# Weight products walked from the last column to the first

## The chip, the cores and the metric

The kernel runs on one core of one Trainium2 chip. The metric is the device time of one execution in microseconds. The kernel before took 2161.43 us as the median of three executions (2161.38 to 2162.55 us).

## The reference

A two-layer decoder trunk on 256 tokens of width 2048, all in float32. With `rms` for the scaled root-mean-square norm, it computes:

```
x = x + NSA(rms(x))                       # 16 heads: compressed, selected and window branch, gated
x = x + square(relu(rms(x) @ up0)) @ down0    # up: 2048 x 8192, down: 8192 x 2048
k, v = rms(x) @ kv_w_shared               # once
x = x + DiffAttn(rms(x) @ w_q, k, v) @ w_out  # softmax minus lambda times softmax
x = x + square(relu(rms(x) @ up1)) @ down1
out = rms(x)
```

Nearly all of its arithmetic is in the products of 256 tokens with weight matrices: 64 MB for each of the four MLP matrices, and 5168, 2048, 1024, 2048 and 2048 columns of 2048 rows for the projections.

## The kernel before, in words

**Split operands.** A float32 operand is held as two float32r tiles, a high part and a low part (`split`, L149: ScalarE copies the high part, VectorE subtracts it from the source). A product is three TensorE products: high by high, high by low, low by high (`mm3`, L144).

**Weights.** `plan` lists the weight matrices in units of 512 rows by 512 columns. A unit is read by two DMAs of 512 KB on SyncE's queue into `raw` tiles (L266) and split into two pairs `wh`, `wl` of 128 partitions x 2 x 512 (L151 and L152). Up to four units are asked for ahead, and two split ahead (`advance`, L283). `raw`, `wh` and `wl` have four buffers each.

**Two product loops use a unit.** `unit_mm` (L296) serves the projections, the two output products and the down products: for each of four row blocks and both token blocks it holds 128 x 128 of the activations stationary and streams 512 weight columns through `mm3`, 24 products of 512 columns in all. They add up in two PSUM tiles of 512 columns, one for each token block. `up_unit` (L709) serves the up products: it holds 128 x 128 of the weights stationary and streams the activations of one row block. Those lie as 256 high and 256 low columns side by side, so the product with `wh` streams 512 columns and that with `wl` the first 256, into the same PSUM tile; a unit has 16 such pairs, over four PSUM tiles.

**What else uses TensorE.** The products of the compression (`cmp_units`, L511), of the gates (L483) and of attention (`nsa_head`, `diff_head`) call `mm` and `mm3` directly. `transpose` (L140) turns tiles against an identity.

**Order.** TensorE's and SyncE's instructions stand in the order in which the program issues them. Attention's steps are put between the weight products by a planner: each `mm` adds `max(o.shape[-1], 256) / 2400.0` us to a model clock (L138), and `tick` starts the next waiting step when its due time has come. PSUM has eight tiles of 512 columns, four named `acc` and four named `tp`.

Of the kernel before, what the change touches and what calls it, by code (L numbers as in the profile page):

```python
# [16 lines left out]
S = 256  # L17
# [14 lines left out]
def kernel(  # L32
# [79 lines left out]
    def tick():  # L112
        if tasks and tasks[0][0] <= clock[0]:
            step()
# [21 lines left out]
    def mm(o, l, r, start, stop, shared=False):  # L136
        nc.tensor.matmul(o, lhsT=l, rhs=r, start=start, stop=stop, skip_group_check=shared)  # L137
        clock[0] += max(o.shape[-1], 256) / 2400.0  # L138

    def transpose(o, i, idn):  # L140
        nc.tensor.transpose(o, i, idn)  # L141
        clock[0] += 0.11

    def mm3(o, lh, ll, rh, rl, start, stop):  # L144
        mm(o, lh, rh, start, False)
        mm(o, lh, rl, False, False)
        mm(o, ll, rh, False, stop)
# [148 lines left out]
    def unit_mm(us, ps, lhs, start, stop, ts_=(0, 1)):  # L296
        for kk in range(4):
            wh, wl = us[kk // 2]
            h, l = lhs(kk)
            for t in ts_:  # L300
                ts = slice(t * P, (t + 1) * P)
                mm3(ps[t], h[:, ts], l[:, ts], wh[:, kk % 2, :], wl[:, kk % 2, :],
                    start and kk == 0, stop and kk == 3)
                tick()

# [18 lines left out]
    def xt_chunk(c, sets):  # L324
        for pr in range(2):
            if pr:
                yield 0.8
            tp = PT("tp")
            for kk in range(2):
                k = pr * 2 + kk  # L330
                for t in range(2):
                    transpose(tp[:, kk * 256 + t * P:kk * 256 + (t + 1) * P],
                                        x[c][:, t, k * P:(k + 1) * P], ident)
            for gf, xt in sets:
                for kk in range(2):
                    k = c * 4 + pr * 2 + kk
                    split(xt[k // 8][:, k % 8, 0, :], xt[k // 8][:, k % 8, 1, :],
                          tp[:, kk * 256:(kk + 1) * 256], gf(k))
# [25 lines left out]
    def transpose_k(src, th, tl):  # L364

        for pr in range(2):
            if pr:
                yield 0.8
            tp = PT("tp")
            for hh in range(2):  # L370
                for t in range(2):
                    h = pr * 2 + hh
                    transpose(tp[:, hh * 256 + t * P:hh * 256 + (t + 1) * P],
                              src[:, t, h * P:(h + 1) * P], ident)
            hs = slice(2 * pr, 2 * pr + 2)
            split(th[:, hs], tl[:, hs], tp.rearrange("p (h t q) -> p h t q", h=2, t=2))
# [19 lines left out]

    tp = PT("tp")
    transpose(tp[:, 0:32], grow_a, ident[0:32, 0:32])
    nc.vector.tensor_copy(gcol, tp[:, 0:32])
    gsub = cp.tile([P, 1], F32, name="gsub")  # L400
# [23 lines left out]
    def proj(xt, between=None, before=None):  # L424
        ps = [PT("acc"), PT("acc")]
        for u in range(4):
            if before is not None:
                drain(before[u])
                tick()
            unit_mm(next_unit(), ps, xtlhs(xt, 4 * u), u == 0, u == 3)  # L430
            if between is not None:
                between(u)
        return ps
# [29 lines left out]
    for j in range(2):  # L463
        ps = proj(xt, before=None if j else xts)
# [46 lines left out]
    def cmp_units(j, cps, first):  # L511
        def f(u):
            drain(tX[j])
            us = next_unit()
            for kk in range(4):
                l = first * 4 + u * 4 + kk
                wh, wl = us[kk // 2]
                mm(cps[0:120, :], X[j][:, l, :], wh[:, kk % 2, :], l == 0, False)
                mm(cps[0:120, :], X[j][:, l, :], wl[:, kk % 2, :], False, l == 31)
                tick()  # L520
        return f
# [57 lines left out]
    for j in range(2):  # L579
        cps = PT("acc")  # L580
        ps = proj(xt, cmp_units(j, cps, 0))
        ready.append(spawn(project_k(ps, kkh[:, :, j::2, :], kkl[:, :, j::2, :])))
        tick()
        ps = proj(xt, cmp_units(j, cps, 4))
# [90 lines left out]
    for g in range(4):  # L675
        ps = proj(xt)
# [11 lines left out]
    def out_proj(oth, otl, sets, ss):  # L688
        done = []
        pss = {}  # L690
        for c, g in out_order():
            while len(line) < 4 * g + 4:
                clock[0] = max(clock[0], tasks[0][0])
                step()
            drain(*line[4 * g:4 * g + 4])
            if (c, g) in OUT_FIRST:
                pss[c] = [PT("acc"), PT("acc")]
            ps = pss[c]
            unit_mm(next_unit(), ps, xlhs(oth, otl, 4 * g), (c, g) in OUT_FIRST, (c, g) in OUT_LAST)
            if (c, g) in OUT_LAST:  # L700
                for t in range(2):
                    nc.vector.tensor_tensor(x[c][:, t, :], x[c][:, t, :], ps[t], ALU.add)
            if g == 3:
                done.append(spawn(xt_chunk(c, sets()), 3.5))
                stat_chunk(ss, c)
        line.clear()
        return done

    def up_unit(us, ps, xt, k0):  # L709


        for pair in range(2):
            for kk in range(4):
                wh, wl = us[kk // 2]
                k = k0 + kk
                both = xt[k // 8][:, k % 8].rearrange("p s q -> p (s q)")
                for b in (2 * pair, 2 * pair + 1):
                    bs = slice(b * P, (b + 1) * P)
                    mm(ps[b], wh[:, kk % 2, bs], both, k == 0, False)
                    mm(ps[b][:, 0:S], wl[:, kk % 2, bs], both[:, 0:S], False, k == 15)  # L720
                tick()

    def mlp(layer, xt, rs, last_hook, before):
        r2 = T([P, 2], "nrs")
        nc.vector.tensor_tensor(r2, rs, rs, ALU.mult)
        for G in range(4):
            hid = []
            for c in range(4):
                ps = [PT("acc" if c % 2 == 0 else "tp") for _ in range(4)]
                for u in range(4):  # L730
                    if G == 0 and c == 0:
                        drain(before[u])
                        tick()
                    up_unit(next_unit(), ps, xt, 4 * u)
                r = T([P, 4, S], "q")
                h = new_kv(2, 4, S)
                for b in range(4):
                    nc.scalar.activation(r[:, b, :], ps[b][:, S:2 * S], AF.Copy)
                    nc.vector.tensor_tensor(r[:, b, :], r[:, b, :], ps[b][:, 0:S], ALU.add)
                    nc.vector.scalar_tensor_tensor(r[:, b, :], r[:, b, :], 0.0, r[:, b, :], ALU.max, ALU.mult)  # L740
                    split(h[:, 0, b, :], h[:, 1, b, :], r[:, b, :])
                hid.append(h)
# [8 lines left out]
            for c, u in down_order(final):  # L751
                if u == 0:
                    tag = "tp" if c >= 2 and G < 3 else "acc"
                    pss[c] = [PT(tag), PT(tag)]
                lhs = xlhs(hid[u][:, 0], hid[u][:, 1], 0)
                if final and c >= 2 and u == 3:
                    kept[c] = (next_unit(), lhs)
                    continue
                unit_mm(next_unit(), pss[c], lhs, u == 0, u == 3)
                if u == 3:  # L760
                    for t in range(2):
                        residual(c, t)
                    if G == 3:
                        last_hook(c)
# [49 lines left out]
    ps = proj(kxt, before=xts)  # L814
# [5 lines left out]
    for d in (dkh, dkl):  # L820
        for cc in range(2):
            r = slice(64 - cc * 64, 128 - cc * 64)
# [19 lines left out]
    ps = proj(kxt)  # L842
# [83 lines left out]
    for g in range(4):  # L926
        ps = proj(dxt)
# [100 lines left out]
```

## Time and profile before

| | |
|---|---|
| median of three executions | 2161.43 us |
| the profiled execution | 2163.18 us |
| span, first to last instruction, of that execution | 2161.4 us |
| TensorE products | 10780 instructions, busy 2133.4 us |
| VectorE, ScalarE, GpSimd busy | 1334.9, 1083.1, 82.4 us |
| read from HBM | 390.47 MB, 182 GB/s over the span |

The span lies inside the execution's own time, which is 1.8 us longer. Busy time of TensorE counts a product from its start to its modelled end, so that products in a row overlap; how fast they follow each other is read from a stretch's length over the count of products in it. The granted clock stands as a share of full speed.

### The profile page before, as it was taken

Reading aid. Unit: us, or ns where it says so; the run is one execution under the profiler, and the core shown is the slowest. Engines: PE = TensorE matmul, PEld = TensorE weight load, DVE = VectorE, ACT = ScalarE, POOL = GpSimd, SP = SyncE. Lnnn points to the kernel's source line nnn. Section 1 sums busy time; section 2 is a strip of 40 time slices with the busy share of each in tenths; the row PEclk is TensorE's granted clock in tenths of the full one; section 3 lists DMA queues with packets and bytes.
Section 4 is the critical chain, followed back from the end, with each engine's and each line's share of the span. In section 5 each row is a group of like instructions: output and inputs, shape, how many; then the busy total and the mean of one; then the engine's idle time right before and its main releaser. Section 6 shows DMA issues by size and latency. Waiting matters only on the chain.

```text
span 2161.4 us, 28803 instructions
## 1 busy us (share of the span) xinstructions
PE 2133.4 (99%) x10780; PEld 1797.2 (83%) x10780; DVE 1334.9 (62%) x2156; ACT 1083.1 (50%) x1737; POOL 82.4 (4%) x121
## 2 busy tenths in 40 slices
PE   8999999999999999999999999999999999999998
PEld 6778888888888888888888877888888888888886
DVE  5666777675546555555666578866555655655654
ACT  6565666464435434434455466655434434534443
POOL 0101100000000000000000111000000000000000
PEclk9999999999999999999999999999999999999999
DMA  7788432456666566566565644466666666666654
GB/s 238 236 264 249 124 102 89 149 175 195 194 188 184 195 194 183 192 193 189 181 194 185 189 142 127 132 192 187 198 192 185 191 194 186 185 195 186 192 190 143
DMA packets 204828, 394.45 MB, mean 183 GB/s; under 512 B 14176, under 2 KB 14368, under 8 KB 204560
## 3 DMA queue, kind: packets, MB, share of 16 engines
q1 hardware_dynamic: 203936, 390.51, 58.2%
q0 software_dynamic: 560, 2.02, 0.3%
q8 instruction: 84, 1.38, 0.3%
q14 instruction: 56, 0.46, 0.1%
q10 hardware_dynamic: 192, 0.08, 0.0%
HBM read 390.47 MB, written 2.10 MB: 182 GB/s over the span
## 4 chain that ended last, share of the span: by engine, by line
PE 92%; DVE 3%; DMA 2%; ACT 1%; issue 1%; POOL 0%; DVEq 0%; SPq 0%; POOLq 0%; ACTq 0%
PE acc L137 57%; PE tp L137 33%; PE tp L141 2%; DVE wl L152 1%; DMA raw<-in_nsa_w_in_dram 1%; DMA raw<-in_nsa_cmp_w_dram 1%; ACT wh L151 1%; ACT sbt L879 0%; ACT sa L879 0%; POOL sq L915 0%; DVE sbt L886 0%; DVE big L155 0%; DVE psl L152 0%; DVE sa L886 0%; DVE pwl L911 0%
## 5 line engine op out<-in xcount | busy, mean ns | idle before, releaser
L152 DVE TENSOR_TENSOR wl<-raw,wh 128x1024 fp32r<-128x1024 f32 x736 | 903.7, 1229 | 712.0 <-ACT wh L151 706.8
L151 ACT ACTIVATE wh<-raw 128x1024 fp32r<-128x1024 f32 x736 | 778.2, 1059 | 827.1 <-PE acc L137 488.0
L137 PE MATMUL acc<-wh,big 128*128 128x512 f32 (+1 forms) x1600 | 542.7, 400 | 1.9 <-ACT wh L151 1.9
L137 PE MATMUL acc<-wh,kv 128*128 128x512 f32 x1280 | 397.0, 390 | 0.0
L137 PE MATMUL tp<-big,wh 128*128 128x512 f32 (+1 forms) x1040 | 362.8, 395 | 0.0
L137 PE MATMUL acc<-big,wh 128*128 128x512 f32 x1024 | 361.7, 397 | 0.0
L137 PEld LDWEIGHTS acc<-wh,big 128*128 128x128 f32 (+1 forms) x1600 | 301.6, 189 | 61.3 <-ACT wh L151 2.3
L137 PE MATMUL acc<-wl,big 128*128 128x512 f32 (+1 forms) x832 | 326.3, 392 | 0.5 <-DVE wl L152 0.5
L137 PE MATMUL tp<-big,wl 128*128 128x256 f32 (+1 forms) x1040 | 289.4, 281 | 0.0
L137 PE MATMUL acc<-big,wl 128*128 128x256 f32 x1024 | 287.4, 281 | 0.0
L137 PEld LDWEIGHTS acc<-wh,kv 128*128 128x128 f32 x1280 | 240.3, 188 | 50.0
L137 PE MATMUL acc<-wl,kv 128*128 128x512 f32 x640 | 249.1, 389 | 0.0
L137 PE MATMUL tp<-wh,kv 128*128 128x512 f32 x768 | 237.4, 389 | 0.0
L137 PEld LDWEIGHTS tp<-big,wh 128*128 128x128 f32 (+1 forms) x1040 | 194.2, 187 | 46.7
L137 PEld LDWEIGHTS acc<-big,wh 128*128 128x128 f32 x1024 | 192.2, 188 | 46.3
L137 PEld LDWEIGHTS tp<-big,wl 128*128 128x128 f32 (+1 forms) x1040 | 195.4, 189 | 0.0
L137 PEld LDWEIGHTS acc<-big,wl 128*128 128x128 f32 x1024 | 193.5, 189 | 0.2
L137 PEld LDWEIGHTS acc<-wl,big 128*128 128x128 f32 (+1 forms) x832 | 157.0, 189 | 28.7 <-DVE wl L152 1.0
L137 PEld LDWEIGHTS tp<-wh,kv 128*128 128x128 f32 x768 | 144.1, 188 | 30.0
L137 PE MATMUL tp<-wl,kv 128*128 128x512 f32 x384 | 149.4, 389 | 0.0
L137 PEld LDWEIGHTS acc<-wl,kv 128*128 128x128 f32 x640 | 120.2, 188 | 24.5
L151 ACT ACTIVATE kv<-q 128x256 fp32r<-128x256 f32 x128 | 50.0, 412 | 73.4 <-DVE q L740 73.4
(183 smaller groups left out, 1418.1 us busy)
## 6 DMA issues: line engine op xcount, KB each, us to landing
raw<-in_mlp_w_up_dram SPq DMA_DIRECT2D x256, 512.0 KB, 3.9
raw<-in_mlp_w_down_dram SPq DMA_DIRECT2D x256, 512.0 KB, 4.3
raw<-in_nsa_w_in_dram SPq DMA_DIRECT2D x80, 512.0 KB, 4.5
raw<-in_nsa_cmp_w_dram SPq DMA_DIRECT2D x32, 512.0 KB, 4.9
raw<-in_nsa_w_out_dram SPq DMA_DIRECT2D x32, 512.0 KB, 3.7
raw<-in_diff_w_q_dram SPq DMA_DIRECT2D x32, 512.0 KB, 3.7
raw<-in_diff_w_out_dram SPq DMA_DIRECT2D x32, 512.0 KB, 3.7
raw<-in_kv_w_shared_dram SPq DMA_DIRECT2D x16, 512.0 KB, 3.6
```

The lines of the kernel that those rows point to most:

```text
L137: nc.tensor.matmul(o, lhsT=l, rhs=r, start=start, stop=stop, skip_group_check=shared)
L141: nc.tensor.transpose(o, i, idn)
L151: nc.scalar.activation(h, src, AF.Copy)
L152: nc.vector.tensor_tensor(l, src, h.bitcast(F32), ALU.subtract)
```

## The change

Two helpers are added, `mmr` and `mmr3`. They are `mm` and `mm3` with the output's and the moving operand's columns in reverse order, by a slice with step -1. `unit_mm` and both lines of `up_unit` call them in place of `mm3` and `mm`. Each product still reads the same columns and writes each to the same place; it begins with the last one. The stationary operands, the counts and shapes, and the model clock's step are the same. The compression, the gates, attention and the transposes keep the ascending order.

```diff
+    def mmr(o, l, r, start, stop):
+
+        mm(o[:, ::-1], l, r[:, ::-1], start, stop)
+
+    def mmr3(o, lh, ll, rh, rl, start, stop):
+        mmr(o, lh, rh, start, False)
+        mmr(o, lh, rl, False, False)
+        mmr(o, ll, rh, False, stop)
@@ unit_mm
-                mm3(ps[t], h[:, ts], l[:, ts], wh[:, kk % 2, :], wl[:, kk % 2, :],
+                mmr3(ps[t], h[:, ts], l[:, ts], wh[:, kk % 2, :], wl[:, kk % 2, :],
                     start and kk == 0, stop and kk == 3)
@@ up_unit
-                    mm(ps[b], wh[:, kk % 2, bs], both, k == 0, False)
-                    mm(ps[b][:, 0:S], wl[:, kk % 2, bs], both[:, 0:S], False, k == 15)
+                    mmr(ps[b], wh[:, kk % 2, bs], both, k == 0, False)
+                    mmr(ps[b][:, 0:S], wl[:, kk % 2, bs], both[:, 0:S], False, k == 15)
```

## Rows read from the trace of the kernel before

**Rows 1.** The page: busy time of each engine, share of the span, instructions.
```profile
PE 2133.4 (99%) x10780; PEld 1797.2 (83%) x10780; DVE 1334.9 (62%) x2156; ACT 1083.1 (50%) x1737; POOL 82.4 (4%) x121
```

**Rows 2.** The page: the chain that ended last, by engine and line.
```profile
PE 92%; DVE 3%; DMA 2%; ACT 1%; issue 1%; POOL 0%; DVEq 0%; SPq 0%; POOLq 0%; ACTq 0%
PE acc L137 57%; PE tp L137 33%; PE tp L141 2%; DVE wl L152 1%; DMA raw<-in_nsa_w_in_dram 1%; DMA raw<-in_nsa_cmp_w_dram 1%; ACT wh L151 1%; ACT sbt L879 0%; ACT sa L879 0%; POOL sq L915 0%; DVE sbt L886 0%; DVE big L155 0%; DVE psl L152 0%; DVE sa L886 0%; DVE pwl L911 0%
```

**Rows 3.** All waits: who waited for whom, us in total, times, longest.
```profile
ACT wh L151 <- PE acc L137: 488.0, 315, 3.4
...
ACT wh L151 <- PE tp L137: 275.1, 173, 3.2
```

**Rows 4.** TensorE's products by form: count | busy us, mean ns | idle before.
```profile
L137 PE MATMUL acc<-wh,big 128*128 128x512 f32 x1536 | 519.7, 400 | 1.9 <-ACT wh L151 1.9
L137 PE MATMUL acc<-wh,kv 128*128 128x512 f32 x1280 | 397.0, 390 | 0.0
L137 PE MATMUL acc<-big,wh 128*128 128x512 f32 x1024 | 361.7, 397 | 0.0
L137 PE MATMUL tp<-big,wh 128*128 128x512 f32 x1024 | 360.8, 397 | 0.0
L137 PE MATMUL acc<-wl,big 128*128 128x512 f32 x768 | 301.1, 392 | 0.5 <-DVE wl L152 0.5
...
L137 PE MATMUL acc<-big,wl 128*128 128x256 f32 x1024 | 287.4, 281 | 0.0
L137 PE MATMUL tp<-big,wl 128*128 128x256 f32 x1024 | 287.4, 281 | 0.0
L137 PE MATMUL acc<-wl,kv 128*128 128x512 f32 x640 | 249.1, 389 | 0.0
...
L137 PE MATMUL tp<-wh,kv 128*128 128x512 f32 x768 | 237.4, 389 | 0.0
...
L137 PE MATMUL tp<-wl,kv 128*128 128x512 f32 x384 | 149.4, 389 | 0.0
```

**Rows 5.** The chain in order of time, MLP stretches: start us, length us, products.
```profile
501.25 22.19 PE acc L137 x128
523.43 22.19 PE tp L137 x128
...
655.30 22.61 PE tp L137 x128
...
723.14 43.54 PE acc L137 x192
```

**Rows 6.** By stretch: length, busy us (count) of each engine, PEclk, DMA share, GB/s.
```profile
0.00:15.00 15.00, 6.88 (x20) 5.06 (x21) 4.76 (x9) 8.44 (x17) 3.11 (x11) 1.00 0.89 303
...
501.25:523.43 22.18, 22.18 (x129) 19.55 (x129) 13.98 (x21) 10.85 (x17) 0.00 (x0) 1.00 0.62 190
...
655.30:677.91 22.61, 22.61 (x130) 19.60 (x129) 14.01 (x21) 10.93 (x17) 0.00 (x0) 1.00 0.63 187
723.14:766.69 43.55, 43.55 (x194) 36.04 (x193) 24.59 (x27) 18.11 (x21) 0.00 (x0) 1.00 0.61 193
```

**Rows 7.** VectorE reading PSUM, by form: in steps of 16 (L451), side by side (L702).
```profile
L702 DVE TENSOR_TENSOR x<-x,acc 128x512 f32<-128x512 f32 x40 | 26.7, 680 | 0.3 <-PE acc L137 0.3
...
L451 DVE TENSOR_TENSOR q<-tp,gcol 128x480 f32<-128x480 f32 x8 | 5.0, 651 | 0.5 <-PE tp L141 0.4
```

**Rows 8.** TensorE in order of time, the first products: start us, us to the end.
```profile
12.54 0.63 PE L137 MATMUL acc<-wl,big 128*128 128x512 f32 x1
12.96 1.05 PE L137 MATMUL acc<-wh,big 128*128 128x512 f32 x2
13.81 0.63 PE L137 MATMUL acc<-wl,big 128*128 128x512 f32 x1
14.24 0.63 PE L137 MATMUL acc<-wh,big 128*128 128x512 f32 x1
```

**Rows 9.** TensorE in order of time, up products: start us, us to the end.
```profile
1000.96 0.40 PE L137 MATMUL acc<-big,wh 128*128 128x512 f32 x1
1001.20 0.28 PE L137 MATMUL acc<-big,wl 128*128 128x256 f32 x1
1001.32 0.40 PE L137 MATMUL acc<-big,wh 128*128 128x512 f32 x1
```

## The prediction

> **What bounds the kernel now.** I read the page's busy times first: TensorE's products cover 2133.4 of 2161.4 us [rows 1]. That alone is weak, because ends of products are modelled. The chain that ended last says it better: 92% of it is TensorE, of which 57% and 33% are products at the helper's line, into the two kinds of PSUM tile [rows 2]. The waits agree: the largest ones of ScalarE's weight split are for TensorE to free a weight buffer, 488.0 and 275.1 us [rows 3]. So the engines that feed TensorE wait for it, and whatever each product costs is paid in full.
>
> What a product costs is read from stretches of the chain, as length over count, not from its 390 to 400 ns of duration [rows 4], which include a tail that overlaps the next one. A group of 192 down products takes 43.54 us, so 226.8 ns for each 512 columns. Up products come in pairs of 512 and 256 columns: 64 pairs take 22.19 us in a layer's first group and 22.61 us in the later ones, 346.7 and 353.3 ns a pair [rows 5]. [...]
>
> **The change part by part.** No instruction is added, removed or moved. The planner's clock takes its step from the number of output columns, which is the same, so attention's steps stay between the same products; DMAs, splits, readers of PSUM and releases of buffers keep their places in every queue. The whole effect is in how long one product takes.
>
> How many are touched: `unit_mm` issues the products whose moving operand is a weight tile, with stationary big or kv: 1536 + 768 + 1280 + 640 + 768 + 384 = 5376 of 512 columns. `up_unit` issues 1024 + 1024 of 512 columns and as many of 256, 2048 pairs [rows 4]. Their present price is 5376 x 0.2268 = 1219 us, and 512 pairs x 0.3467 + 1536 pairs x 0.3533 = 720 us (a quarter of the pairs lie in first groups), 1939 us together. That is 90% of the span, the same share that the chain gives to that line [rows 2]. So a change of 1% in a touched product is 19 us.
>
> *The read.* The moving operand is a run of 512 or 256 adjacent values of each partition, before and after; only its direction turns. No product of this trace reads downwards. The nearest rows on an address walk that isn't plain are VectorE's: a sum that reads PSUM in steps of 16 takes 651 ns for 480 values, 1.36 ns each, and one that reads 512 adjacent values of PSUM takes 680 ns, 1.33 ns each [rows 7]. A walk far from plain cost 2% there, on an engine with a slower stream. I take 0 for the read.
>
> *The write.* Each product writes and adds the same adjacent PSUM columns, downwards. [...] Between ends so far apart I take 0, by the nearest row of an odd PSUM walk [rows 7].
>
> [...]
>
> *Neighbours.* Both products of an up pair go to one PSUM tile, and the three of an `mm3` too. The order in each is the same in both, so between two writes of one column lie 512 columns as before, except in an up pair: column 255 was written 512 columns before its second write and now 256. The second product begins 0.24 us after the first, whose end is put 0.16 us later still, at 0.40 us [rows 9]; now too it starts on columns before the first product's end, so nothing here waits for an earlier sum. I cost it at 0, though the distance is halved; if the second had to wait for the first one's end, that would be 2048 x 0.16 = 330 us.
>
> Sum: 0 us. The profiled execution of 2163.2 us stays 2163.2 us. It lies 1.75 us above the median, so for the median I forecast 2161.4 us.
>
> **The rivals.**
>
> *Half the column rate (slower).* If TensorE's path to PSUM, or its read, handles two columns at a time only when the second lies above the first, every touched product falls to one column in two cycles. [...] Against it: the columns stay adjacent, and the four-product row [rows 8] shows this rate only at the start. It decides wherever TensorE sets the pace, 90% of the chain. [...]
>
> *A fixed price for each turned product (slower).* The stream itself keeps its rate, but the start of a descending walk, or the hand-over between products, costs some cycles. [...] Against it: forward products too begin at an address far from where the last one ended. [...] With the wait for an up pair's first product above, 2490 us.
>
> [...]
>
> *The change does nothing.* The slices could be turned back to ascending order on the way to the chip, since both operands are reversed together. The time is then that of the forecast, and the trace alone would not tell the two apart; a kernel that turns only one of the two operands would.
>
> **How the numbers follow.** No change, for either reason: 0.52. Half rate: 0.27, since the stream has no slack and no row shows a write that isn't plain. A fixed price: 0.13. Faster: 0.08. What a measurement of this kernel can tell from no change is about 0.2%, 4.3 us; the chances are faster 0.08, within 0.52, slower 0.40. The likeliest case's own range is 2157 to 2166 us. To leave out no more than 2 in 10 the range must reach over the half rate: 2150 to 3850 us. Left out are the gains beyond 11 us and the upper end of the half rate, some 0.1.
>
> **What would show it.** In the profile after: 43.5 us for 192 down products and 22.2 or 22.6 us for 128 up products in the chain, with the same counts. At half rate 192 products take about 82 us, ScalarE's waits for TensorE grow in step, and DMA falls from 187 to near 100 GB/s in the MLP [rows 6]; products of attention and transposes keep their durations. A fixed price shows as the same number of ns on pairs' both products, whatever their columns. A shift in the order of the instructions, or new waits of TensorE, would mean that the second part's first paragraph is wrong. The forecast fails if a stretch of turned products differs by over 0.5% from its twin before.

## The result, and the profile after

The changed kernel takes 2194.65 us (median of five, 2193.61 to 2195.28) against 2161.38 us of the kernel before (median of five): a ratio of 1.0152, 95% interval 1.0140 to 1.0165, 33 us slower. I had forecast no change.

The profiled execution has a span of 2192.4 us. Its page, busy times and chain that ended last:

```profile
PE 2168.4 (99%) x10780; PEld 1800.1 (82%) x10780; DVE 1334.4 (61%) x2156; ACT 1082.9 (49%) x1737; POOL 80.9 (4%) x121
...
PE 95%; DVE 2%; ACT 1%; issue 1%; DMA 1%; POOL 0%; SPq 0%; DVEq 0%; POOLq 0%; ACTq 0%
```

Beside [rows 1, 2] the count of TensorE's products is the same; busy time grew by 35.0 us, and TensorE's share of the chain from 92% to 95%. The order of the instructions is the same on every engine. So the products themselves became longer. The chain in order of time (start us, length us, products) has the same stretches as [rows 5]:

```profile
482.32 22.61 PE tp L137 x128
...
662.37 22.61 PE tp L137 x128
...
730.21 44.80 PE acc L137 x192
```

A group of 192 down products takes 44.80 us and no longer 43.54: 233.3 ns for 512 columns, 6.6 ns more. Up pairs take 353.3 ns in every group: the first groups lost their 346.7 ns, the later ones have the same mean as before. The clock is not the reason: the row of the down stretch reads 1.00, as in [rows 6].

```profile
730.21:775.01 44.80, 44.80 (x194) 36.10 (x193) 24.65 (x27) 18.11 (x21) 0.00 (x0) 1.00 0.61 187
```

By form, the products that read a weight tile are longer than in [rows 4], those of 256 columns not:

```profile
L137 PE MATMUL acc<-wh,kv 128*128 128x512 f32 x1280 | 406.6, 398 | 0.0
...
L137 PE MATMUL acc<-big,wl 128*128 128x256 f32 x1024 | 285.8, 279 | 0.0
```

The mean rose from 390 to 398 ns for the first and went from 281 to 279 ns for the second. The waits moved in step [rows 3]: ScalarE's splits wait 509.7 and 284.0 us for TensorE, 30.6 us more together.

```profile
ACT wh L160 <- PE acc L137: 509.7, 320, 3.4
ACT wh L160 <- PE tp L137: 284.0, 174, 3.2
```

The sum: 5376 products x 6.6 ns = 35 us, and eight stretches of 64 up pairs in the first groups x 0.42 us = 3.4 us, 39 us. The medians differ by 33 us. Between 5 and 6 us hide, most of it in the first 480 us, where TensorE also waits for weights: the first whole stretch of up products begins at 482.32 us and before at 479.06, only 3.3 us later, though 56 units x 24 products x 6.6 ns = 8.9 us of price lie ahead of it.

### The profile page after: what moved, and what is told of

It reads as the page before. It is cut to its first block, busy times and chain, and to the rows that moved or that the text cites. A ratio compares the mean times of both kernels' runs of the same rounds, so it can differ in the third digit from the quotient of the medians.

```text
span 2192.4 us, 28806 instructions
## 1 busy us (share of the span) xinstructions
PE 2168.4 (99%) x10780; PEld 1800.1 (82%) x10780; DVE 1334.4 (61%) x2156; ACT 1082.9 (49%) x1737; POOL 80.9 (4%) x121
## 4 chain that ended last, share of the span: by engine, by line
PE 95%; DVE 2%; ACT 1%; issue 1%; DMA 1%; POOL 0%; SPq 0%; DVEq 0%; POOLq 0%; ACTq 0%
PE acc L137 60%; PE tp L137 33%; PE tp L145 2%; DVE wl L161 1%; DMA raw<-in_nsa_w_in_dram 1%; ACT wh L160 0%; ACT sa L888 0%; ACT sbt L888 0%; POOL sq L924 0%; DVE psl L161 0%; DVE big L164 0%; DVE sbt L895 0%; DVE pwl L920 0%; DVE pwl L926 0%; DVE sa L895 0%
## 5 line engine op out<-in xcount | busy, mean ns | idle before, releaser
L160 ACT ACTIVATE wh<-raw 128x1024 fp32r<-128x1024 f32 x736 | 777.4, 1058 | 855.6 <-PE acc L137 509.7
L137 PE MATMUL acc<-wh,big 128*128 128x512 f32 (+1 forms) x1600 | 551.0, 406 | 1.2 <-ACT wh L160 1.2
L137 PE MATMUL acc<-wh,kv 128*128 128x512 f32 x1280 | 406.6, 398 | 0.0
L137 PE MATMUL acc<-wl,big 128*128 128x512 f32 (+1 forms) x832 | 331.7, 399 | 0.5 <-DVE wl L161 0.5
L137 PE MATMUL acc<-wl,kv 128*128 128x512 f32 x640 | 254.3, 397 | 0.0
L137 PE MATMUL tp<-wh,kv 128*128 128x512 f32 x768 | 243.2, 397 | 0.0
L137 PEld LDWEIGHTS tp<-wl,kv 128*128 128x128 f32 x384 | 72.2, 188 | 17.4
```

Source lines behind the costliest of these rows:

```text
L160: nc.scalar.activation(h, src, AF.Copy)
```

## Experiments

**Which of the two directions: one at a time.** `mmr` turns only the output in one kernel (the first new line), and only the moving operand in another (the second); both leave the product's columns mirrored.

```diff
-        mm(o[:, ::-1], l, r[:, ::-1], start, stop)
+        mm(o[:, ::-1], l, r, start, stop)
+        mm(o, l, r[:, ::-1], start, stop)
```

> Only the product is written downwards; the moving operand is read upwards, so each weight product's columns come out mirrored (the values are not the reference's). Write theory (the descending PSUM write costs one step of 6.6 ns for each product of 512 columns): 192 down products take 44.8 us, 64 up pairs 22.6 us in the first group too, 2194 us. Read theory (the descending read costs it): 43.54 us for 192 down products, 22.19 us in the first up group, 2161 us. If each direction costs a part: between, 2170 to 2185 us.

> Only the moving operand is read downwards; the product is written upwards, so the columns come out mirrored here too. Read theory: 44.8 us for 192 down products, 2194 us. Write theory: 43.54 us and 2161 us. If it takes a mismatch of the two directions to be slow, both this and the kernel with only the write turned are slow and the changed kernel would have had to be fast, which it is not.

Writing down alone: 2161.45 us against 2161.11 us of the kernel before, ratio 1.000 (0.9991 to 1.0009). Reading down alone: 2193.79 us, ratio 1.0148 (1.0133 to 1.0163). The chains, writing down first:

```profile
476.12 22.19 PE tp L137 x128
...
542.68 43.56 PE acc L137 x192
```

```profile
484.77 22.61 PE tp L137 x128
...
552.62 44.80 PE acc L137 x192
```

The write has no price that these runs can see, the read has the whole of it. A mismatch of the two directions is not the cause either: writing down alone is such a mismatch and costs nothing, and the changed kernel has none and is slow. That settles the main question; the rest asks what of the read costs.

**Where the operands lie.** 32 bytes are put ahead of all tiles. As I count the layout, weight and activation tiles then begin at a multiple of 128 bytes and no longer 96 past one; no trace shows an address.

```diff
+    shift = cp.tile([P, 8], F32, name="shift")
+    nc.gpsimd.memset(shift, 0.0)
     cst = cp.tile([P, 640], F32, name="cst")
```

> The kernel before with 32 bytes put ahead of all tiles, so that moving and stationary tiles begin at a multiple of 128 bytes in place of 96 past one. Address theory (a product's surplus depends on where in an aligned stretch of memory the walk begins; upwards it begins 96 past a multiple of 128, downwards 92): the spacing of down products moves by one step of 6.6 ns from 226.8 ns, to 220 or 233 ns, which is 2130 or 2197 us. Write and read theories (the direction itself costs it): 226.8 ns and 2161 us.

> The changed kernel with the same 32 bytes ahead of all tiles: the descending read begins 124 past a multiple of 128 bytes in place of 92. Address theory: the spacing of down products leaves 233.3 ns, to 226.7 ns or less (2161 us) or 240 ns. Write and read theories: 233.3 ns and 2194 us as without the shift.

Shifted and ascending: 2160.95 us, ratio 0.9995 (0.9985 to 1.0005). Shifted and descending: 2193.57 us, ratio 1.0146 (1.0130 to 1.0161). The first down stretch of each:

```profile
542.91 43.56 PE acc L137 x192
```

```profile
550.29 44.80 PE acc L137 x192
```

The address theory falls, for this shift.

**The order of the walk.** All else ascending, the eight groups of down products take the columns in eight orders, each for read and write alike.

```diff
+        if blk == 1:
+            return ap[:, ::-1]
+        return ap.rearrange("p (a b) -> p a b", b=blk)[:, ::-1, :]
...
+            walk[0] = (256, 64, 16, "alternate", 4, 2, 1, 8)[layer * 4 + G]
```

> Only the down products differ from the kernel before; each of their eight groups (four of each layer) walks its 512 columns, in the read and the write alike, in another order: blocks of 256, 64, 16 columns taken from the last block to the first with ascending columns inside; every second product descending and the next ascending; blocks of 4; of 2; wholly descending; blocks of 8. Read from the length of 192 down products in the chain (43.54 us ascending, 44.80 us descending). Start theory (the price is for a walk that begins at the end of its range or with a downward step): all block groups 43.5 us, the wholly descending one 44.8 us, the alternating one half way, 44.2 us. Stream theory (each downward step over a border of a memory line costs a little, and the sum shows once it passes a threshold): blocks of 256 and 64 stay at 43.5 us, 16, 8 and 4 cost as much as or more than the wholly descending walk. Hand-over theory (the price is for the jump from one product's last address to the next one's first): the alternating group has no jumps and is at 43.5 us or below.

One execution, 2169.28 us. The chain, with blocks of 256, 64 and 16, an up stretch behind the latter, the alternating group (90 products), and the wholly descending walk (blocks of 4 and 2 take the same 44.8 us):

```profile
543.99 43.56 PE acc L160 x192
...
721.51 43.55 PE acc L160 x192
...
899.01 44.80 PE acc L160 x192
...
988.62 22.18 PE acc L137 x128
...
1106.09 20.90 PE acc L160 x90
...
1890.09 44.80 PE acc L160 x192
```

Blocks of 256 and 64 are free; blocks of 16 and below cost just what the wholly descending walk does (for 8, in the last group: 84.02 us for the last 360 products, the same as in the changed kernel). The start theory falls: a walk in blocks of 16 begins with an ascending run. The hand-over theory, as I had put it, falls too: the alternating group was to be at 43.5 us or below, and takes 232.2 ns a product. The same 90 products take 227.1 ns in the kernel before, in this row, and 233.4 ns (21.01 us) in the changed kernel:

```profile
1106.29 20.44 PE acc L137 x90
```

That is four fifths of the price for half of the descending products. The test is a weak one, though, since successive products mostly read different tiles (`wh`, `wl`, `wh`), and a jump from tile to tile stays. The stream theory foretold which blocks cost something; why 31 downward steps cost the same as 511 it does not say.

The 988.62 row shows something that I had not looked for: up products, ascending, are at the fast 22.2 us behind a slow down group, and in this run at the slow 22.6 us behind a fast one (22.61 us from 653.67 us on). I come back to it below.

**How many columns.** The down products read and write only the first n columns (all but the first product of each sum; the others are left out), descending in one kernel and ascending in its twin.

```diff
+            walk[0] = ((496, -1), (480, -1), (448, -1), (416, -1), (384, -1), ...)[layer * 4 + G]
```

> Only the down products differ from the kernel before: they read and write the first 496, 480, 448, 416 (layer 0) and 384, 320, 256, 512 columns (layer 1) alone, reading them downwards and writing upwards; all but the first product of each sum leave the remaining columns out. Start theory: the spacing is the ascending one of the same count of columns plus 6.6 ns at each count. Stream theory: the price shrinks with the count, 6.6 ns at 512 and none at 256.

> The twin of the kernel with short down products, the same columns left out, read upwards. [...]

One execution each, 2057.13 and 2048.35 us. The chains for 496, 448 and 384 columns, descending and then ascending (480 columns take 42.30 and 41.66 us):

```profile
542.76 43.55 PE acc L156 x192
...
891.94 39.79 PE acc L156 x192
...
1502.40 34.36 PE acc L156 x192
```

```profile
543.23 42.91 PE acc L156 x192
...
893.25 39.04 PE acc L156 x192
...
1501.30 33.55 PE acc L156 x192
```

Over 192 products the price at 496, 480, 448 and 384 columns is 3.3, 3.3, 3.9 and 4.2 ns each, against 6.6 ns at 512 columns. It halves with the first 16 columns left out, because the ascending products gain little by them: from 512 to 496 columns an ascending product gets 3.3 ns shorter (226.8 to 223.5 ns) and a descending one 6.5 ns (233.3 to 226.8 ns), and from 496 to 448 columns 20.2 and 19.6 ns. At 320 columns TensorE in order of time shows the next `wl` product, three products on, after 0.44 us in both (descending first), so no price:

```profile
1690.66 0.31 PE L156 MATMUL tp<-wl,kv 128*128 128x320 f32 x1
...
1691.10 0.31 PE L156 MATMUL tp<-wl,kv 128*128 128x320 f32 x1
```

```profile
1690.19 0.31 PE L156 MATMUL tp<-wl,kv 128*128 128x320 f32 x1
...
1690.63 0.31 PE L156 MATMUL tp<-wl,kv 128*128 128x320 f32 x1
```

So it is neither the same at every count, as the start theory had it, nor proportional to the count. I first read this as a spacing that goes in steps of 6.6 ns, into which a small delay is rounded. No run shows that, and the order of time speaks against it. Up pairs of the kernel before, at the slow pace of 353.3 ns, don't each take 6.6 ns more than the fast ones; their second products follow each other after 0.34, 0.36 and 0.36 us, and so on:

```profile
1000.50 0.28 PE L137 MATMUL acc<-big,wl 128*128 128x256 f32 x1
...
1000.84 0.28 PE L137 MATMUL acc<-big,wl 128*128 128x256 f32 x1
...
1001.20 0.28 PE L137 MATMUL acc<-big,wl 128*128 128x256 f32 x1
...
1001.56 0.28 PE L137 MATMUL acc<-big,wl 128*128 128x256 f32 x1
```

The two paces are means of patterns over several products. What makes the patterns stays open.

**Steps of 2 and 4.** Down products of 256 columns two apart, of 128 four apart, up and down; and 504, 508, 464, 352 adjacent columns descending; the remaining columns are left out.

> Only the down products differ: they read 256 columns in steps of 2 upwards and downwards, 128 in steps of 4 upwards and downwards (layer 0), and 504, 508, 464, 352 adjacent ones downwards (layer 1), the remaining columns left out. If the read works line by line with a price for each line: 256 columns in steps of 2 touch the same lines as 512 adjacent ones and take clearly more than 120 ns. If only the count of columns counts: 120 ns for 256. Start theory: downwards always 6.6 ns above upwards. Stream theory: 504 and 508 cost as 512 does, 352 costs nothing.

One execution, 2109.18 us. The chain for steps of 2 upwards and downwards:

```profile
543.62 43.92 PE acc L156 x192
...
722.20 44.80 PE acc L156 x192
```

256 columns two apart take 228.8 ns in this stretch, as long as 512 adjacent ones and not 120 ns; downwards there are 4.6 ns on top. That looks as if the memory that a read passes over were paid, but the steps of 4 say otherwise. 128 columns four apart pass over as much, and at a granted clock of 1.00 three of these products (upwards) take 0.35 us, 118 ns each in the 87 from 901.44 to 911.69 us:

```profile
905.00:910.00 5.00, 5.00 (x45) 5.00 (x44) 4.68 (x6) 3.19 (x4) 0.00 (x0) 1.00 0.67 210
905.33 0.30 PE L156 MATMUL acc<-wl,kv 128*128 128x128 f32 x1
...
905.68 0.30 PE L156 MATMUL acc<-wl,kv 128*128 128x128 f32 x1
```

For each column read that is 0.44 ns for adjacent columns, 0.89 ns two apart and at most 0.92 ns four apart: a step doubles the price of a column here, and a longer one adds little. A descending walk of adjacent columns stays near 0.46 ns. So neither theory of the read, a price for each line or for the count alone, holds.

504, 508 and 464 columns descending take 229.0, 231.7 and 211.6 ns. They have no ascending twins, nor have the 352 columns, so their price isn't known.

Later in this group the granted clock fell to 0.50, just before 916 us, behind a wait of TensorE for the split of a weight unit of 1.61 us and at the start of another of 0.90 us:

```profile
915.37 0.36 PE L156 MATMUL acc<-wh,kv 128*128 128x128 f32 x1 [1.61 <-ACT wh L171]
...
913.00:916.00 3.00, 1.11 (x8) 0.73 (x6) 0.66 (x1) 1.40 (x2) 0.00 (x0) 0.99 0.92 347
...
916.70:930.00 13.30, 13.30 (x63) 13.30 (x63) 9.66 (x9) 6.84 (x8) 0.00 (x0) 0.50 0.74 252
```

Most of the downward steps of 4 ran at that clock, and I read nothing from them.

**Which products, and blocks of 32.** Only some of the down products descend.

```diff
+        if walk[0] is not None and walk[0](seen[0], kind, t):
...
+            walk[0] = (lambda n, kind, t: 32, lambda n, kind, t: kind == 0, lambda n, kind, t: kind == 1, None, lambda n, kind, t: kind == 2, lambda n, kind, t: n % 24 == 1, lambda n, kind, t: n % 12 == 1, None)[layer * 4 + G]
```

Here `n` counts the products of a group, and `kind` is 0, 1 or 2 for high by high, high by low and low by high. 32 stands for blocks of 32. A product for which the rule is false ascends.

> Only down products differ from the kernel before: the walk takes blocks of 32 columns from the last to the first (group 1 of layer 0), or ascends but for one product in three, the high by high one or the high by low one (groups 2 and 3), or the low by high one, one in 24, one in 12 (layer 1). Per-product price (each descending product pays 6.6 ns for itself): one in three 43.96 us for 192 products, one in 24 43.57 us. Step theory (the stream's spacing goes in steps of 6.6 ns, a descending product needs some 3 ns more, and the rounding up falls on its neighbours too): one in three costs more than a third of the 1.26 us, and the three kinds need not agree. Blocks of 32: 43.54 us if a run of 32 still counts as ascending, 44.80 us otherwise.

One execution, 2168.43 us. The chain in the order of the diff, without the two ascending groups:

```profile
544.43 44.61 PE acc L155 x192
...
724.10 44.39 PE acc L137 x192
...
901.61 43.95 PE acc L137 x192
...
1535.65 44.39 PE acc L137 x192
...
1714.86 43.57 PE acc L137 x192
...
1892.44 43.63 PE acc L137 x192
```

One descending product in three costs 0.85 us in 192 when it is the high by high or the low by high one, 13 ns for each of the 64; 0.41 us, 6.4 ns, when it is the high by low one. One in 24 costs 0.03 us in these 192, 4 ns each, and one in 12 0.09 us, 6 ns each. So each of the two theories fits a part: one in 24, one in 12 and the high by low rows agree roughly with a price for each descending product, while the other two cost twice that, as a theory in which neighbours pay too would have it. The alternating group fits the latter as well. Blocks of 32 cost 5.6 ns of the 6.6: the border between free and paid lies between runs of 32 and of 64 columns.

**The changed kernel with ascending up products.**

```diff
-                    mmr(ps[b], wh[:, kk % 2, bs], both, k == 0, False)
-                    mmr(ps[b][:, 0:S], wl[:, kk % 2, bs], both[:, 0:S], False, k == 15)
+                    mm(ps[b], wh[:, kk % 2, bs], both, k == 0, False)
+                    mm(ps[b][:, 0:S], wl[:, kk % 2, bs], both[:, 0:S], False, k == 15)
```

> The changed kernel with the up products ascending again; the 5376 products whose moving operand is a weight tile still descend. If the price lies in these and the up products gain where they follow a descending group: 44.8 us for 192 down products, 22.19 us in every up group, 2162 + 35 - 10 = 2183 to 2187 us, less what hides. If up products have their own pace: 22.61 us in the later groups, 2190 us.

2180.37 us, ratio 1.0088 (1.0071 to 1.0105), 3 us below the expected span of times: 35 - 10 us, less the 5 us that hide. A down stretch and the up stretch behind it:

```profile
594.40 44.80 PE tp L137 x192
639.20 22.19 PE acc L137 x128
```

Beside the changed kernel's 2194.65 us this says one thing more: in these groups descending up pairs take 353.3 ns and ascending ones 346.7, so the up products pay for their direction in every group, some 14 us. That the later groups took 353.3 ns before the change too, ascending, hid it.

**What sets the pace of the up products.** Only the last 1, 24, 96 products of a down group (layer 0) or the last 3, 6, 2 (layer 1) descend.

> Everything ascends as in the kernel before, but for the last products of some down groups: the last 1, 24 and 96 of a group's 384 descend in the first three groups of layer 0, the last 3, 6 and 2 in those of layer 1. Carried-state theory (the up products' pace, 22.19 or 22.61 us for 64 pairs, is left over from how the stream ran just before them, and one late step sets it): the up groups behind them run at 22.19 us wherever the count of late steps is right, perhaps behind all, and the whole takes some 2155 us. Own-cause theory (the pace of an up group has its reason in the whole group before it or in its own operands): 22.61 us behind the short tails of 1, 2, 3 and 6, 22.19 us at most behind 96; 2161 us.

One execution, 2153.32 us. The first up stretch behind the last 1, the last 3 and the last 2 (behind the last 24, 96 and 6 it is 22.19 us too):

```profile
630.50 22.60 PE acc L137 x128
...
1614.57 22.19 PE acc L137 x128
...
1966.23 22.19 PE acc L137 x128
```

Two descending products ahead of an up group decide at which of two paces all of its 256 ascending pairs run (each tail stands ahead of one group of this one execution). The carried-state theory holds, but for the single late product. Descending products as such are not the rule, though. Behind the groups of 384 columns it is the other way round: the up stretch is slow behind the descending ones (first row) and fast behind the ascending ones:

```profile
1571.12 22.60 PE acc L137 x128
```

```profile
1568.40 22.19 PE acc L137 x128
```

The carried state leads to a version of its own, with six:

```diff
+                cs = slice(None, None, -1) if turn and kk == 3 else slice(None)
+                mm3(ps[t][:, cs], h[:, ts], l[:, ts], wh[:, kk % 2, cs], wl[:, kk % 2, cs],
...
+                unit_mm(next_unit(), pss[c], lhs, u == 0, u == 3, turn=G < 3 and (c, u) == (3, 3))
```

> The kernel before, in which only the last six of the 384 down products descend, in the six down groups that an up group follows. Carried-state theory: all up groups at 22.19 us for 64 pairs, 24 chunks of 64 pairs each 0.42 us shorter, 10.1 us in all, against 36 descending products at up to 6.6 ns, 0.2 us: some 2151 us, ratio 0.995. Own-cause theory: up groups at 22.61 us, 2161 us.

2151.11 us against 2161.45, ratio 0.9956 (0.9943 to 0.9970): faster than both kernels. Every up group is at 22.19 us:

```profile
630.55 22.19 PE acc L137 x128
...
1004.43 22.19 PE tp L137 x128
```

## Why the prediction was wrong

- *What bounds the kernel* held: TensorE's stream, with the price of each product paid nearly in full; of 39 us some 33 appear.
- *No instruction added, removed or moved* held: the same order on every engine, no new wait of TensorE.
- *The read at 0* failed. It is the step that the forecast hung on. I took it from a VectorE row [rows 7], an engine whose stream says little about how TensorE's products follow each other. Measured, a descending read costs 6.6 ns for each of the 5376 products of 512 weight columns and for each pair of the first up groups: 39 us, of which 33 appear.
- *The write at 0* held by luck, for the reason was as weak: writing down alone changes nothing, within 0.1% (2161.45 us against 2161.11).
- *The neighbours at 0* held: with the write alone turned, which halves the distance between the two writes as well, 64 up pairs of the first group kept 22.19 us; the wait of 0.16 us is not there. That up pairs of the later groups kept 353.3 ns in the changed kernel is no evidence, since there a dearer read replaced a slow pace.
- *Half the rate* did not come: 233.3 ns for 512 columns, far from the 425 ns of the first four products [rows 8], the pace that the upper end of my range, 3850 us, stands for and that no run shows for a turned product. That the stream has no slack, as the chance of 0.27 has it, no run shows; measured, a column took 0.46 ns read downwards and 0.44 ns upwards. Only walks with a step took twice the time for each column, 0.89 ns two apart and at most 0.92 ns four apart.
- *A fixed price for each turned product* is what came, the rival with a chance of 0.13: 6.6 ns a product of 512 weight columns. A hint of it was in the profile before: the same pairs at 346.7 and at 353.3 ns [rows 5], at a granted clock of 1.00 [rows 6]. I did not ask what sets the two paces, which differ by just what a turned product came to cost. Its name is right only for 512 columns: at 320 three products take 0.44 us in both directions. Its sign, the same number of ns on both products of a pair, did not come either: a first-group pair grew by 6.6 ns as a whole, as much as one product of 512 columns.
- *Faster*, with a chance of 0.08, did not come with this change. The version with six descending products won 10 us, as many as 1536 later pairs at the first groups' pace save (1536 x 6.6 ns).

Settled: it is the read's direction (6.6 ns a product) and not the write's (2161.45 us against 2161.11); not the tiles' place, for a shift of 32 bytes (43.56 and 44.80 us as without it); and it is paid by walks whose ascending runs are of 32 columns (44.61 us) or of 16 and less (44.80 us). Open: why a run of 64 is free (43.55 us), why a descending read costs anything, whether in the stream or between products, and what holds the stream at one of two paces. No run here looks inside the operand read.

## What to carry to other kernels

Where a stream of products sets the time, take its spacing from a stretch's length over the count, and compare stretches of the same products: two paces at one clock are a sign that something small, here the order in which a few products read, costs or wins some 2%. With 512 float32r columns, let TensorE read its moving operand in ascending runs of at least 64 columns: here 192 products took 43.55 us with runs of 64 and 44.61 us with runs of 32. The write's direction was free (43.56 us). When one direction of access changes on both sides, time each side alone before looking for a cause in both. A price of 0 taken from another engine's row is a guess, and is best called one.

## What the runs showed of the hardware that I had not expected

- 256 float32r columns two apart take 228.8 ns a product, as many as 512 adjacent ones (226.8 ns), at a granted clock of 1.00; 128 columns four apart take 118 ns, so it isn't the memory passed over that is paid.
- The same ascending up pairs run at 346.7 or at 353.3 ns for all 256 pairs of a group, depending on the products ahead of them; six products read and written the other way round in each of six groups won 10 us.
- A product of 512 weight columns took 226.8 ns ascending and 233.3 ns descending, and means between (228.9 and 231.2 ns) when one product in three descended. The first 16 columns left out saved 6.5 ns descending and only 3.3 ns ascending.
- The granted clock fell to 0.50 behind a wait of TensorE of 1.61 us and at the start of one of 0.90 us, and it stayed there from 916.70 to 930.00 us though products of 128 columns four apart covered the whole of that stretch.
